# Two up-projections of a scan get buffers of their own; readout weights and gated outputs move to the ring of the scans' loads

## The chip, the core and the metric

The kernel runs on one core of one Trainium2 chip. The metric is device time in microseconds (us) of one execution. Engines: PE is TensorE, DVE VectorE, ACT ScalarE, POOL GpSimd, SP SyncE, which here issues nearly all DMA transfers, in its program's order.

## The reference

Two blocks on 256 tokens of width 2048, in float32, batch 1. The first block is two layers of attention (four kinds of head groups). The second, which the change lies in, is one trunk layer: the latent tokens (x) and 256 context tokens (c) are projected with the same weights, a pair of recurrent branches reads both, their results are merged, and an MLP follows.

```
h  = modulate(rms_norm_2(x, norm1_w), sh1, sc1)
hc = modulate(rms_norm_2(ctx, norm1_w), csh1, csc1)
p, pc = h @ in_w, hc @ in_w[:, :A_COLS + B_COLS]
pa, pb, pg = split_cols(p, [A_COLS, B_COLS, GATE_COLS])
ya = rwkv7_branch(pa, pca, ...)      # 16 heads of 64
yb = gdn_branch(pb, pcb, ...)        # 8 heads of 128, gated delta rule
x = x + g1 * merge_branches(ya, yb, pg, up_a, up_b, out_w)
x = x + g2 * squared_relu_mlp(modulate(rms_norm_2(x, norm2_w), sh2, sc2), mlp_w1, mlp_w2)

def rwkv7_prepare(z, w0, w_up, a0, a_up, k_k, k_a):
    ...
    tw = jnp.tanh(xw)
    for d in range(2):
        w = -jax.nn.softplus(-(w0[d] + tw @ w_up[d])) - 0.5
        a = jax.nn.sigmoid(a0[d] + xa @ a_up[d])
        k_d = k * (1.0 + (a - 1.0) * k_a)
    ...

def merge_branches(ya, yb, pg, up_a, up_b, out_w):
    gate_a, gate_b = jnp.split(jax.nn.sigmoid(pg), 2, axis=-1)
    return (gate_a * (ya @ up_a) + gate_b * (yb @ up_b)) @ out_w
```

Each scan goes over the context first and hands its state to the scan over x; only the scans over x give an output. `w_up` and `a_up` (here `wup` and `aup`) are the two up-projections of the RWKV branch. An RWKV output is normalised per head with `ln_w` and `ln_b` and multiplied by a gate from `g_up`; a gated output is normalised per head and gated.

## The kernel before, in words

All weights of the projections are streamed: `load_w` (L140) loads tiles `wr` of 512 KB into three buffers, ACT splits each into a rounded part `wh` (L230) and DVE the rest `wl` (L231), and PE multiplies them with the activations in three products (L171 to L173, in PSUM tiles `pp`). These matmuls fill PE for nearly the whole time.

The scans run beside the projections. There are twelve, each a Python generator: four RWKV scans on c (`rwkv`, four heads each), two gated ones on c (`gdn`, also four heads each), then four and two on x. `scans` keeps two of them going at a time, in two slots, and takes the next when one ends. The four RWKV scans on x are called x0 to x3 in this document. The projection of the gates and `up_a` (the multiplication of `ya` with its up-projection) come at the end of the stretch in which the scans run, then `merge`, which begins with loading the gated result `ytb` from DRAM (L1711). Each branch's output goes to DRAM: `yad` (L1455) for RWKV, from where `up_a` loads it as `yk` (L1699), `ybd` (L1652) for the gated one.

The order of the instructions on each engine is not written by hand. A scheduler places them by priority (the scans' is raised by 4000 against that of the code beside them) and by its own estimate of times. A tile name with several buffers is a ring: a new tile takes a buffer that is free, and its first write, here the load on SP, waits until the last reader of what lay there is done. SP issues in its program's order, so whatever stands behind such a load waits as well.

The ring "p2" has N2 = 5 buffers of 128x512 float32. An RWKV scan takes from it k2, v2, on x also r2 (in the trace `k`, `v` and `r`), `wup` and `aup`; a gated scan takes two `gvt` and a `gsq`. All loads of `_load` stand on L1405, whatever asked for them. Each (direction, head pair) of an RWKV scan multiplies first with `wup` (L1233), then with `aup` (L1234). L1221 transposes v2; L1273 makes `kr` from k2 and r2, and is their last reader.

The name "lg" has one buffer of 128x1024. The readout of an RWKV scan on x puts its normalisation weights (`ln`) and `gup` there; a gated scan on x gathers its output there as `gosb` (L1610 to L1641), from which L1649 transposes head by head, L1651 multiplies with the gate (`go`), and L1652 stores.

Of the kernel before, what the change touches and what calls it, by code (L numbers as in the profile page):

```python
# [13 lines left out]
AF = mybir.ActivationFunctionType  # L14
# [3 lines left out]
MUL, ADD, SUB = ALU.mult, ALU.add, ALU.subtract  # L18
# [11 lines left out]
N1, N2, NM = 6, 5, 4  # L30
# [20 lines left out]
def bc(ap, n, axis):  # L51

    l = [list(x) for x in ap.ap]
    l.insert(axis, [0, n])
    return bass.AP(tensor=ap.tensor, offset=ap.offset, ap=l)
# [787 lines left out]
class Second:  # L843
# [337 lines left out]
    def rwkv(self, b, src):  # L1181
        e, nc, a = self.e, self.e.nc, self.a
        v, s, g = nc.vector, nc.scalar, nc.gpsimd
        mm, tr = nc.tensor.matmul, nc.tensor.transpose
# [4 lines left out]
        f256 = slice(256 * b, 256 * b + 256)  # L1189
        ld = lambda n, ap: self._load(n, ap, "p2")  # L1190
        k2, v2 = ld("k2", zd[:, 8 + t0:10 + t0, :]), ld("v2", zd[:, 16 + t0:18 + t0, :])
        r2 = ld("r2", zd[:, t0:t0 + 2, :]) if isx else None
        wu = ld("wup", a["wup"][:, :, f256].rearrange("d p c -> p d c"))
        au = ld("aup", a["aup"][:, :, f256].rearrange("d p c -> p d c"))
        cols = lambda n: pv[n][:, t0:t0 + 2]

        hk, ok, hkk = (e.t([128, 2], n, 2) for n in ("hk", "ok", "hkk"))
# [6 lines left out]
        p = e.pt()  # L1204
        for t in range(2):
            sq = e.t([128, T], "sq", N1, tag="p1")
# [11 lines left out]
        p = e.pt()  # L1218
# [9 lines left out]
        for t in range(2):  # L1228
            fs = []
            for d in range(2):  # L1230
                p = e.pt()
# [31 lines left out]
                f = e.t([128, T], "rf", N1, tag="p1")  # L1263
# [6 lines left out]
            if isx:  # L1270
# [3 lines left out]
                f = e.t([128, T], "rf", N1, tag="p1")  # L1274
# [138 lines left out]
    def rwkv_readout(self, b, yT, bo, vn):  # L1413
        e, nc, a = self.e, self.e.nc, self.a
        v, s, g = nc.vector, nc.scalar, nc.gpsimd
        lg = e.t([128, 2, 2, 256], "lg", 1)
        ln, gup = lg[:, 0], lg[:, 1]
        for n in range(2):
            nc.sync.dma_start(ln[:, n], bc(a[("lnw", "lnb")[n]][256 * b:256 * b + 256], 128, 0))
        nc.sync.dma_start(gup, a["gup"][:, :, 256 * b:256 * b + 256])  # L1420
        p = e.pt()
        py = p.rearrange("p (i t r c) -> p i t r c", i=2, t=2, r=2)
        for i in range(2):
            for t in range(2):
                nc.tensor.transpose(py[:, i, t].rearrange("p r c -> p (r c)"), yT[:, t, i, :], e.ident)
        y = e.t([128, 2, 2, 2, 64], "ynat", NN, tag="nat")
        m = e.t([128, 2, 2, 2], "ym", 1)
        v.tensor_reduce(m, py, axis=AX.X, op=ADD)
        f3 = lambda x: x.rearrange("p i t r -> p (i t r)")
        v.tensor_scalar(f3(m), f3(m), 1.0 / 64, None, op0=MUL)  # L1430
        yf = y.rearrange("p i t r c -> p (i t r) c")
        v.tensor_tensor(yf, p.rearrange("p (u c) -> p u c", c=64), bc(f3(m), 64, 2), op=SUB)
        sq = e.t([128, 8, 64], "ysq", NN, tag="nat")
        s.activation(sq, yf, AF.Square)
        ss = e.t([128, 8], "yss", 1)
        v.tensor_reduce(ss, sq, axis=AX.X, op=ADD)
        r = e.t([128, 8], "yrs", 1)
        e.rsqrt(r, ss, [128, 8], "y", 1.0 / 64, 64e-5)
        v.tensor_tensor(yf, yf, bc(r, 64, 2), op=MUL)
        y2 = y.rearrange("p i t r c -> p i (t r c)")  # L1440
        v.tensor_tensor(y2, y2, bc(ln[:, 0], 2, 1), op=MUL)
        v.tensor_tensor(y2, y2, bc(ln[:, 1], 2, 1), op=ADD)
        v.tensor_tensor(sq, vn.rearrange("p i t (r c) -> p (i t r) c", r=2), bc(f3(bo), 64, 2), op=MUL)
        v.tensor_tensor(yf, yf, sq, op=ADD)
        for t in range(2):
            p = e.pt()
            for k in range(2):
                nc.tensor.matmul(p[:, :T], gup[:, k, t * 128:(t + 1) * 128], self.xg[:, k, :], start=k == 0, stop=k == 1)
            for i in range(2):
                nc.tensor.transpose(p[:, T + i * 128:T + (i + 1) * 128], y[:, i, t].rearrange("p r c -> p (r c)"), e.ident)  # L1450
            gt = e.t([128, T], "rgt", N1, tag="p1")
            s.copy(gt, p[:, :T])
            o = e.t([128, T], "ro", N1, tag="p1")
            v.tensor_tensor(o, p[:, T:], gt, op=MUL)
            nc.sync.dma_start(self.ya[:, 2 * b + t, :], o)  # L1455
# [35 lines left out]
    def gdn(self, b, src):  # L1491
# [81 lines left out]
        S = e.t([128, 2, 4, 128], "gst", 2, tag="vs")  # L1573
        if isx:
            nc.sync.dma_start(S, self.gstd[b])
            osb = e.t([128, 2, 4, 128], "gosb", 1, tag="lg")
        cc = lambda h: slice(h * 128, h * 128 + 128)
        p3 = lambda p: p.rearrange("p (h c) -> p h c", h=4)
        for j in range(2):
            blk = (j, 1 - j)  # L1580
            first = not isx and j == 0
            for d in range(2):
                i = blk[d]
                c = slice(i * 128, (i + 1) * 128)
                col = lambda x, h: x[:, i, d * 8 + h0 + h:d * 8 + h0 + h + 1]
                if isx:
                    at = self._load("gatl", self.at[:, d, b * 8 + i * 4:b * 8 + i * 4 + 4, :], "mk")
                if first:
                    rhs = vn[:, i]
                else:  # L1590
                    p = e.pt()
                    for h in range(4):
                        mm(p[:, cc(h)], kq[:, h, 0, c], S[:, d, h, :], start=True, stop=True)
                    rhs = e.t([128, 4, 128], "grhs", 1, tag="ysb")
                    for h in range(4):
                        v.scalar_tensor_tensor(rhs[:, h], p[:, cc(h)], col(negeg, h), vn[:, i, h], op0=MUL, op1=ADD)
                p = e.pt()
                for h in range(4):
                    mm(p[:, cc(h)], nt[:, d, i * 4 + h, :], rhs[:, h], start=True, stop=True)
                y = e.t([128, 4, 128], "gyy", NM, tag="mk")  # L1600
                v.tensor_tensor(y, p3(p), bc(m[:, i, d], 128, 2), op=MUL)
                if isx:
                    pa, pb = e.pt(), e.pt()
                    for h in range(4):
                        mm(pa[:, cc(h)], kq[:, h, 1, c], S[:, d, h, :], start=True, stop=True)
                        mm(pb[:, cc(h)], at[:, h], y[:, h], start=True, stop=True)
                    o = osb[:, i]
                    t1 = o if j == 0 else e.t([128, 4, 128], "gt1", NN, tag="nat")
                    for h in range(4):
                        s.activation(t1[:, h], pa[:, cc(h)], AF.Copy, scale=col(eg, h))  # L1610
                    if j:
                        v.tensor_tensor(o, o, t1, op=ADD)
                    v.tensor_tensor(o, o, p3(pb), op=ADD)
                if not (isx and j):
                    y2 = e.t([128, 4, 128], "gy2", NN, tag="nat")
                    v.tensor_tensor(y2, y, bc(ee[:, i, d * 8 + h0:d * 8 + h0 + 4], 128, 2), op=MUL)
                    p = e.pt()
                    for h in range(4):
                        mm(p[:, cc(h)], kn[:, i, h], y2[:, h], start=True, stop=True)
                    if first:  # L1620
                        s.copy(S[:, d], p3(p))
                    else:
                        for h in range(4):
                            v.scalar_tensor_tensor(S[:, d, h], S[:, d, h], col(gend, h), p[:, cc(h)], op0=MUL, op1=ADD)
                yield
# [3 lines left out]

        qn = e.t([128, 2, 4], "gqn", 1, tag="ym")  # L1630
        v.tensor_scalar(f2(qn), f2(rn[:, 1]), 128 ** -0.5, None, op0=MUL)
        of = osb.rearrange("p i h c -> p (i h) c")
        v.tensor_tensor(of, of, bc(f2(qn), 128, 2), op=MUL)
        os_ = e.t([128, 8], "gos", 1, tag="yss")
        for i in range(2):
            sq = e.t([128, 4, 128], "gsq2", NN, tag="nat")
            s.activation(sq, osb[:, i], AF.Square)
            v.tensor_reduce(os_[:, i * 4:i * 4 + 4], sq, axis=AX.X, op=ADD)
        r = e.t([128, 8], "gor", 1, tag="yrs")
        e.rsqrt(r, os_, [128, 8], "go", 1.0 / 128, EPS)  # L1640
        v.tensor_tensor(of, of, bc(r, 128, 2), op=MUL)  # L1641
        gw = e.t([128, 1], "ggw", 1)
        v.tensor_scalar(gw, self.pv["gnw"], 0.5, None, op0=MUL)
        for h in range(4):
            gt = e.t([128, T], "ggt", N1, tag="p1")
            nc.sync.dma_start(gt, self.gz[:, h0 + h, :])
            p = e.pt()
            for i in range(2):
                tr(p[:, i * 128:(i + 1) * 128], osb[:, i, h], e.ident)  # L1649
            o = e.t([128, T], "go", N1, tag="p1")  # L1650
            v.scalar_tensor_tensor(o, p[:, :T], gw, gt, op0=MUL, op1=MUL)  # L1651
            nc.sync.dma_start(self.yb[:, h0 + h, :], o)  # L1652
# [285 lines left out]
```

## Time and profile before

| | |
|---|---|
| median of 3 runs | 3415.12 us (3408.39 to 3417.45) |
| the profiled execution | 3419.12 us, its span 3417.4 us |
| PE busy | 3287.1 us (96%) |
| DVE busy | 2360.5 us (69%) |
| ACT busy | 1591.9 us (47%) |
| granted PE clock, mean | 0.975 of 2.4 GHz |
| the chain that ended last | PE 83%, DMA 9%, DVE 5% |

The time of the profiled execution is its span and 1.7 us around it. Busy shares are sums over the span; the chain is followed back from the last instruction, at each step to what released it. The rows on which the prediction rests stand below.

### The profile page before, as it was taken

Reading aid. Unit: us, or ns where it says so; the run is one execution under the profiler, and the core shown is the slowest. Engines: PE = TensorE matmul, PEld = TensorE weight load, DVE = VectorE, ACT = ScalarE, POOL = GpSimd, SP = SyncE. Lnnn points to the kernel's source line nnn. Section 1 sums busy time; section 2 is a strip of 40 time slices with the busy share of each in tenths; the row PEclk is TensorE's granted clock in tenths of the full one; section 3 lists DMA queues with packets and bytes.
Section 4 is the critical chain, followed back from the end, with each engine's and each line's share of the span. In section 5 each row is a group of like instructions: output and inputs, shape, how many; then the busy total and the mean of one; then the engine's idle time right before and its main releaser. Section 6 shows DMA issues by size and latency. Waiting matters only on the chain.

```text
span 3417.4 us, 76977 instructions
## 1 busy us (share of the span) xinstructions
PE 3287.1 (96%) x30462; PEld 3015.2 (88%) x30462; DVE 2360.5 (69%) x5128; ACT 1591.9 (47%) x3191; POOL 352.9 (10%) x635
## 2 busy tenths in 40 slices
PE   8999999999999999999989989999989999999998
PEld 6878889878789898989988889999888989899987
DVE  7757766567577697978887677577767555556655
ACT  4444455443444564635444244245345545445553
POOL 1101000001011030201111103002020000001000
PEclk9999999999999998989999998999999999999999
DMA  7676776876765562535444244255555785555554
GB/s 251 219 257 236 258 233 209 270 263 202 258 206 170 188 191 86 161 100 166 146 151 151 77 146 143 79 174 173 158 189 196 246 272 188 188 188 183 184 189 154
DMA packets 224822, 640.73 MB, mean 187 GB/s; under 512 B 24330, under 2 KB 79948, under 8 KB 224332
## 3 DMA queue, kind: packets, MB, share of 16 engines
q1 hardware_dynamic: 224460, 635.81, 56.9%
q8 instruction: 239, 3.92, 0.5%
q14 instruction: 123, 1.01, 0.1%
HBM read 607.78 MB, written 27.93 MB: 186 GB/s over the span
## 4 chain that ended last, share of the span: by engine, by line
PE 83%; DMA 9%; DVE 5%; issue 1%; ACT 1%; POOL 0%; SPq 0%; DVEq 0%; ACTq 0%
PE pp L173 16%; PE pp L171 16%; PE pp L172 16%; PE pp L166 7%; DMA mw<-in_mod_w 4%; PE pp L167 4%; PE mps L891 3%; PE pp L204 2%; PE pp L203 2%; PE pp L205 2%; DVE wl L231 2%; DMA wup<-in_wup 1%; PE sm L1291 1%; PE sm L1321 1%; PE sm L1333 1%
## 5 line engine op out<-in xcount | busy, mean ns | idle before, releaser
L231 DVE TENSOR_TENSOR wl<-wr,wh 128x512 fp32r<-128x512 f32 x1752 | 1220.8, 703 | 690.3 <-ACT wh L230 664.1
L230 ACT CAST wh<-wr 128x512 fp32r<-128x512 f32 x1752 | 1075.5, 619 | 1300.3 <-PE pp L172 831.9
L171 PE MATMUL pp<-act,wh 128*128 128x256 f32 x3920 | 1133.2, 290 | 19.3 <-ACT wh L230 10.3
L173 PE MATMUL pp<-act,wl 128*128 128x256 f32 x3920 | 1130.1, 289 | 2.4 <-DVE wl L231 2.4
L172 PE MATMUL pp<-act,wh 128*128 128x256 f32 x3920 | 1129.1, 288 | 0.0
L171 PEld LDWEIGHTS pp<-act,wh 128*128 128x128 f32 x3920 | 759.8, 194 | 44.5 <-ACT wh L230 16.0
L173 PEld LDWEIGHTS pp<-act,wl 128*128 128x128 f32 x3920 | 759.1, 194 | 21.5 <-issue 9.7
L172 PEld LDWEIGHTS pp<-act,wh 128*128 128x128 f32 x3920 | 760.4, 194 | 12.6 <-issue 8.5
L173 PE MATMUL pp<-mhi,wl 128*128 128x258 f32 x1024 | 291.5, 285 | 0.0
L171 PE MATMUL pp<-mhi,wh 128*128 128x258 f32 x1024 | 290.4, 284 | 0.0
L172 PE MATMUL pp<-mlo,wh 128*128 128x258 f32 x1024 | 288.5, 282 | 0.0
L166 PE MATMUL pp<-act,wh 128*128 128x512 f32 x752 | 266.0, 396 | 0.0
L167 PE MATMUL pp<-act,wl 128*128 128x256 f32 x768 | 212.4, 280 | 0.8 <-DVE wl L231 0.8
L171 PEld LDWEIGHTS pp<-mhi,wh 128*128 128x128 f32 x1024 | 194.6, 190 | 4.5 <-ACT wh L230 3.7
L173 PEld LDWEIGHTS pp<-mhi,wl 128*128 128x128 f32 x1024 | 193.2, 189 | 4.1 <-issue 4.1
L172 PEld LDWEIGHTS pp<-mlo,wh 128*128 128x128 f32 x1024 | 194.5, 190 | 0.5 <-issue 0.4
L166 PEld LDWEIGHTS pp<-act,wh 128*128 128x128 f32 x752 | 141.2, 188 | 31.6
L166 PE MATMUL pp<-u,wh 128*128 128x512 f32 x480 | 168.2, 392 | 0.0
L167 PEld LDWEIGHTS pp<-act,wl 128*128 128x128 f32 x768 | 144.7, 188 | 4.6 <-DVE wl L231 1.7
L891 PE MATMUL mps<-mw,scw 128*32 128x256 f32 x1536 | 121.7, 390 | 17.9 <-DMA mw<-in_mod_w 17.6
L167 PE MATMUL pp<-u,wl 128*128 128x256 f32 x512 | 138.0, 280 | 0.0
L166 PEld LDWEIGHTS pp<-u,wh 128*128 128x128 f32 x480 | 90.1, 188 | 20.2
(529 smaller groups left out, 4631.4 us busy)
## 6 DMA issues: line engine op xcount, KB each, us to landing
wr<-in_in_w SPq DMA_DIRECT2D x252, 512.0 KB, 4.1
wr<-in_w SPq DMA_DIRECT2D x240, 512.0 KB, 4.6
mw<-in_mod_w SPq DMA_DIRECT2D x192, 512.0 KB, 6.0
wr<-in_w1m SPq DMA_DIRECT2D x128, 512.0 KB, 4.0
wr<-in_w2m SPq DMA_DIRECT2D x128, 512.0 KB, 3.5
wr<-in_wo SPq DMA_DIRECT2D x64, 512.0 KB, 4.5
wr<-in_out_w SPq DMA_DIRECT2D x32, 512.0 KB, 3.2
wr<-in_up_a SPq DMA_DIRECT2D x16, 512.0 KB, 3.2
```

Source lines behind the costliest of these rows:

```text
L166: mm(o, hi, h[2][:, k, :], start=k == 0, stop=False)
L167: mm(o[:, :T], lo, h[0][:, k, :], start=False, stop=False)
L171: mm(o, hi, h[0][:, k, :], start=k == 0, stop=False)
L172: mm(o, hi, h[1][:, k, :], start=False, stop=False)
L173: mm(o, lo, h[0][:, k, :], start=False, stop=k == nk - 1)
L203: mm(p[b], x, hi, start=k == 0, stop=False)
L204: mm(p[b], x, wlo, start=False, stop=False)
L205: mm(p[b], xl, hi, start=False, stop=k == nk - 1)
L230: self.nc.scalar.copy(hi, sl)
L231: self.nc.vector.tensor_tensor(lo, sl, hi, op=SUB)
L891: nc.tensor.matmul(ps[32 * j:32 * j + 32], self.scw[:, k, :], w[:, j * 256:(j + 1) * 256], start=k == 0, stop=k == NK - 1, tile_position=( ...
L1291: mm(p4(p)[:, d, t, :], bT[rows[r], t, d, ch[i]], ar[rows[r], t, d, 0, ch[i]], start=True, stop=True)
```

## The change

`wup` and `aup` leave the ring "p2": each gets a name of its own with one buffer. The shared tile "lg" goes. `ln` and `gup` become two tiles of the ring "p2", and `gosb` two tiles of 128x512 of that ring, one for each half of the tokens. The two multiplies over all of `gosb` (before L1633 and L1641) become two each, on half the size. N2 stays 5.

```diff
--- before.py
+++ after.py
@@ -1190,8 +1190,8 @@
         ld = lambda n, ap: self._load(n, ap, "p2")
         k2, v2 = ld("k2", zd[:, 8 + t0:10 + t0, :]), ld("v2", zd[:, 16 + t0:18 + t0, :])
         r2 = ld("r2", zd[:, t0:t0 + 2, :]) if isx else None
-        wu = ld("wup", a["wup"][:, :, f256].rearrange("d p c -> p d c"))
-        au = ld("aup", a["aup"][:, :, f256].rearrange("d p c -> p d c"))
+        wu = self._load("wup", a["wup"][:, :, f256].rearrange("d p c -> p d c"))
+        au = self._load("aup", a["aup"][:, :, f256].rearrange("d p c -> p d c"))
         cols = lambda n: pv[n][:, t0:t0 + 2]
 
         hk, ok, hkk = (e.t([128, 2], n, 2) for n in ("hk", "ok", "hkk"))
@@ -1413,8 +1413,7 @@
     def rwkv_readout(self, b, yT, bo, vn):
         e, nc, a = self.e, self.e.nc, self.a
         v, s, g = nc.vector, nc.scalar, nc.gpsimd
-        lg = e.t([128, 2, 2, 256], "lg", 1)
-        ln, gup = lg[:, 0], lg[:, 1]
+        ln, gup = (e.t([128, 2, 256], n, N2, tag="p2") for n in ("ln", "gup"))
         for n in range(2):
             nc.sync.dma_start(ln[:, n], bc(a[("lnw", "lnb")[n]][256 * b:256 * b + 256], 128, 0))
         nc.sync.dma_start(gup, a["gup"][:, :, 256 * b:256 * b + 256])
@@ -1573,7 +1572,7 @@
         S = e.t([128, 2, 4, 128], "gst", 2, tag="vs")
         if isx:
             nc.sync.dma_start(S, self.gstd[b])
-            osb = e.t([128, 2, 4, 128], "gosb", 1, tag="lg")
+            osb = [e.t([128, 4, 128], f"gosb{i}", N2, tag="p2") for i in range(2)]
         cc = lambda h: slice(h * 128, h * 128 + 128)
         p3 = lambda p: p.rearrange("p (h c) -> p h c", h=4)
         for j in range(2):
@@ -1604,7 +1603,7 @@
                     for h in range(4):
                         mm(pa[:, cc(h)], kq[:, h, 1, c], S[:, d, h, :], start=True, stop=True)
                         mm(pb[:, cc(h)], at[:, h], y[:, h], start=True, stop=True)
-                    o = osb[:, i]
+                    o = osb[i]
                     t1 = o if j == 0 else e.t([128, 4, 128], "gt1", NN, tag="nat")
                     for h in range(4):
                         s.activation(t1[:, h], pa[:, cc(h)], AF.Copy, scale=col(eg, h))
@@ -1629,16 +1628,17 @@
 
         qn = e.t([128, 2, 4], "gqn", 1, tag="ym")
         v.tensor_scalar(f2(qn), f2(rn[:, 1]), 128 ** -0.5, None, op0=MUL)
-        of = osb.rearrange("p i h c -> p (i h) c")
-        v.tensor_tensor(of, of, bc(f2(qn), 128, 2), op=MUL)
+        for i in range(2):
+            v.tensor_tensor(osb[i], osb[i], bc(qn[:, i], 128, 2), op=MUL)
         os_ = e.t([128, 8], "gos", 1, tag="yss")
         for i in range(2):
             sq = e.t([128, 4, 128], "gsq2", NN, tag="nat")
-            s.activation(sq, osb[:, i], AF.Square)
+            s.activation(sq, osb[i], AF.Square)
             v.tensor_reduce(os_[:, i * 4:i * 4 + 4], sq, axis=AX.X, op=ADD)
         r = e.t([128, 8], "gor", 1, tag="yrs")
         e.rsqrt(r, os_, [128, 8], "go", 1.0 / 128, EPS)
-        v.tensor_tensor(of, of, bc(r, 128, 2), op=MUL)
+        for i in range(2):
+            v.tensor_tensor(osb[i], osb[i], bc(r[:, i * 4:i * 4 + 4], 128, 2), op=MUL)
         gw = e.t([128, 1], "ggw", 1)
         v.tensor_scalar(gw, self.pv["gnw"], 0.5, None, op0=MUL)
         for h in range(4):
@@ -1646,7 +1646,7 @@
             nc.sync.dma_start(gt, self.gz[:, h0 + h, :])
             p = e.pt()
             for i in range(2):
-                tr(p[:, i * 128:(i + 1) * 128], osb[:, i, h], e.ident)
+                tr(p[:, i * 128:(i + 1) * 128], osb[i][:, h], e.ident)
             o = e.t([128, T], "go", N1, tag="p1")
             v.scalar_tensor_tensor(o, p[:, :T], gw, gt, op0=MUL, op1=MUL)
             nc.sync.dma_start(self.yb[:, h0 + h, :], o)
```

The change moves instructions on every engine in the stretch of the scans, since the scheduler decides anew. Three places:

SP's queue around the load of x1's up-projections, from the program of before. `zx` are columns of the projection on their way to the scans, `gstd` is a state that a gated context scan stores, k_28806 is the k2 of x2; what a row waits for stands in brackets, by engine or DMA queue.

```order
L987 DMA zx<-zsh 128x256 [waits DMAHW7_49,DVE_49]
L140 DMA wr<-in_in_w 128x1024 [waits DMAHW4_49,DMAHW0_49,DVE_49]
L1627 DMA gstd_13484<-gst 128x1024 [waits DMAHW1_49,DVE_49]
L1405 DMA wup<-in_wup 97x2x256 [waits DMAHW2_49,DVE_49]
L1405 DMA aup<-in_aup 128x2x256
L1405 DMA k_28806<-zx 128x512 [waits PE_49]
L140 DMA wr<-in_in_w 128x1024 [waits DMAHW5_49,DVE_49]
```

The same place after the change; r_27370 is x1's own r2.

```order
L1405 DMA r_27370<-zx 128x512 [waits DMAHW7_49,DMAHW4_49,PE_49]
L140 DMA wr<-in_in_w 128x1024 [waits DMAHW3_49,DVE_49]
L140 DMA wr<-in_in_w 128x1024 [waits DMAHW5_49,DVE_49]
L140 DMA wr<-in_in_w 128x1024 [waits DMAHW0_49,DVE_49]
L987 DMA zx<-zsh 128x256 [waits DVE_49]
L140 DMA wr<-in_in_w 128x1024 [waits DMAHW6_49,DMAHW2_49,DVE_49]
L140 DMA wr<-in_in_w 128x1024 [waits DMAHW3_49,DVE_49]
L1405 DMA wup<-in_wup 97x2x256 [waits PE_49]
L1405 DMA aup<-in_aup 128x2x256 [waits DMAHW1_49,PE_49]
```

Before, `wup` waits for an instruction of DVE (L1273 of x0); now it waits for one of PE, the last L1233 of x0. From that one to x1's first L1233 PE has 197 matmuls in the old order and 217 in the new. For x3 the release was PE's L1221 of x3 itself, 36 matmuls ahead of the first L1233, and is now x2's last L1233, 325 ahead.

PE's queue at the end of up_a and the begin of the merge, before the change. `act` is `ya` and `yb` the gated result, both split into parts; `pp` are the projections.

```order
L171 MATMUL pp<-act_32233,wh 128x256
L172 MATMUL pp<-act_32233,wh 128x256
L173 MATMUL pp<-act_32233,wl 128x256
L1649 MATMUL sm<-ident,gosb 128x128 x8
L171 MATMUL pp<-yb_32876,wh 128x256 x3
L172 MATMUL pp<-yb_32876,wh 128x256
```

The last transposes of the second gated scan after the change:

```order
L171 MATMUL pp<-act_32243,wh 128x256
L1649 MATMUL sm<-ident,gosb_32010 128x128
L1649 MATMUL sm<-ident,gosb_32011 128x128
L172 MATMUL pp<-act_32243,wh 128x256
L173 MATMUL pp<-act_32243,wl 128x256
L171 MATMUL pp<-act_32236,wh 128x256
```

Before, the merge's first matmul on `yb` stands right behind the last transpose; now 122 matmuls of up_a stand between the two.

SP's queue where up_a's input is loaded, before the change; `ua` takes the gates from DRAM:

```order
L1032 DMA gated<-zsh 128x256
L1699 DMA yk<-yad 128x256 x2
L1687 DMA ua_32241<-gated 128x256
L1699 DMA yk<-yad 128x256 x2
L1405 DMA gatl<-atd 128x512
L1699 DMA yk<-yad 128x256 x4
```

And after it:

```order
L1646 DMA ggt<-gzd 128x256
L1652 DMA ybd<-go 128x256
L1687 DMA ua_32250<-gated 128x256
...
L1646 DMA ggt<-gzd 128x256
L1652 DMA ybd<-go 128x256
L1687 DMA ua_32251<-gated 128x256
L1699 DMA yk<-yad 128x256
L1646 DMA ggt<-gzd 128x256
L1699 DMA yk<-yad 128x256 x2
L1652 DMA ybd<-go 128x256
```

The loads of `yk` now stand among the gate loads (`ggt`) and stores (`ybd`) of the first gated scan on x, which before stood behind them.

## Rows read from the trace of the kernel before

**Rows 1.** The page: the span, and each engine's busy time and share.
```profile
span 3417.4 us, 76977 instructions
PE 3287.1 (96%) x30462; PEld 3015.2 (88%) x30462; DVE 2360.5 (69%) x5128; ACT 1591.9 (47%) x3191; POOL 352.9 (10%) x635
```

**Rows 2.** PE's waits, 1100 to 2520 us: us in total, times, longest.
```profile
PE sm L1233 <- DMA wup<-in_wup: 25.4, 4, 9.4
PE pp L171 <- DMA ytb<-ybd: 13.3, 1, 13.3
PE pp L171 <- ACT wh L230: 6.5, 2, 3.9
...
PE pp L171 <- ACT act L305: 4.4, 1, 4.4
...
PE pp L171 <- DVE ua L1688: 1.8, 1, 1.8
```

**Rows 3.** Busy time, clock and DMA share by stretch of the span.
```profile
core 0: us, PE busy (x) PEld busy (x) DVE busy (x) ACT busy (x) POOL busy (x), PEclk, DMA share, GB/s
1713.20:1738.90 25.70, 25.70 (x217) 25.48 (x215) 24.70 (x76) 14.71 (x31) 3.98 (x5) 1.00 0.50 164
...
1748.40:1758.50 10.10, 10.10 (x40) 8.99 (x40) 5.12 (x17) 1.08 (x4) 0.00 (x0) 0.50 0.13 50
1758.50:1768.60 10.10, 10.10 (x87) 9.90 (x87) 9.21 (x28) 6.84 (x17) 0.00 (x0) 1.00 0.27 82
...
1988.20:2030.90 42.70, 42.68 (x350) 42.21 (x348) 37.02 (x98) 25.23 (x54) 0.00 (x0) 1.00 0.61 189
...
2039.90:2058.90 19.00, 19.00 (x77) 17.02 (x78) 9.60 (x30) 4.05 (x10) 0.00 (x0) 0.50 0.10 35
...
2510.60:2516.30 5.70, 5.67 (x26) 5.67 (x27) 4.01 (x11) 2.23 (x7) 0.00 (x0) 0.50 0.09 32
```

**Rows 4.** Timeline of SP's queue in x1 and x3: start us, us, issue.
```profile
1736.06 0.25 SPq L1405 DMA_DIRECT2D wup<-in_wup  x1
1736.36 5.80 SPq L1405 DMA_DIRECT2D aup<-in_aup  x1
...
2027.30 0.28 SPq L1405 DMA_DIRECT2D wup<-in_wup  x1
```

**Rows 5.** Timeline of DVE, just before that load in x1.
```profile
1735.56 0.47 DVE L1273 SCALAR_TENSOR_TENSOR kr<-k,pv,r 128x256 f32<-128x256 f32 x1
```

**Rows 6.** Timeline of PE around L1233; idle time before and its releaser in brackets.
```profile
1162.28 1.22 PE L1233 MATMUL sm<-twec,wup 97*128 97x256 f32 x2 [5.88 <-DMA wup<-in_wup]
...
1712.55 0.59 PE L1233 MATMUL sm<-twex,wup 97*128 97x256 f32 x2
...
1748.37 2.05 PE L1233 MATMUL sm<-twex,wup 97*128 97x256 f32 x4 [9.42 <-DMA wup<-in_wup]
...
2025.85 0.63 PE L1221 MATMUL sm<-ident,v 128*128 128x128 f32 x4
...
2039.86 1.62 PE L1233 MATMUL sm<-twex,wup 97*128 97x256 f32 x3 [8.98 <-DMA wup<-in_wup]
```

**Rows 7.** The tile `aup`: its issues on SP, ns shortest/median/longest.
```profile
L1405 SPq DMA_DIRECT2D aup<-in_aup x8: 385/5186/6548, 1149.2 to 2033.4; - x8
```

**Rows 8.** Timeline of PE where the merge begins.
```profile
2496.51 0.83 PE L1649 MATMUL sm<-ident,gosb 128*128 128x128 f32 x4 [1.27 <-DVE go L1651]
2510.63 1.01 PE L171 MATMUL pp<-yb,wh 128*128 128x256 f32 x3 [13.29 <-DMA ytb<-ybd]
```

**Rows 9.** The tile `gosb`: durations in ns, shortest/median/longest.
```profile
L1613 DVE TENSOR_TENSOR gosb<-gosb,sm x8: 666/688/689, 2392.9 to 2481.6; 128x512 f32<-128x512 f32 x8
...
L1633 DVE TENSOR_TENSOR gosb<-gosb,gqn x2: 1219/1222/1226, 2419.9 to 2482.8; 128x1024 f32<-128x1024 f32 x2
L1641 DVE TENSOR_TENSOR gosb<-gosb,gor x2: 1225/1226/1226, 2433.5 to 2493.3; 128x1024 f32<-128x1024 f32 x2
```

## The prediction

> **What bounds the kernel now.** I read the page first. TensorE (PE) is busy for 3287.1 of 3417.4 us [rows 1], so all its idle time together is 130 us, and a change that leaves its matmuls alone can only win part of that, and what the low clock after an idle spell costs. Then I asked for PE's waits in the stretch of the scans alone, 1100 to 2520 us [rows 2]. The reader is to see which tiles this change can touch: 25.4 us in four waits for `wup`, 13.3 us in one wait for `ytb`, the load of the gated rule's result at the start of the merge, and, in a row of PE's timeline, 1.27 us for `go`, the step before its store [rows 8]. That is 40.0 us. Third, one row for each stretch of the clock [rows 3]. After each long wait the granted clock is 0.50, which is 1.2 of 2.4 GHz: PE issues 40 matmuls in the 10.10 us behind the second wait and 87 in the next 10.10 us, at 1.00. So a wait costs itself and about half of the slow stretch behind it.
>
> **Why `wup` comes late.** Call the latent scans x0 to x3. In x1 the issue of `wup` stands at 1736.06 us [rows 4], right after `kr` (L1273) of x0, at 1735.56 us [rows 5]. `kr` is the last reader of k2 and r2, and `wup` needs a buffer of the ring "p2" that one of these holds. PE comes to x1's first L1233 and sits 9.42 us, until 1748.37 us [rows 6]; from issue to use that is 12.31 us. x0's own last use of its `wup` was over at 1712.55 + 0.59 = 1713.14 us [rows 6]: the weights wait not for their own predecessor but for the ring. In x3 the same: `wup` issued at 2027.30 us [rows 4] behind the transposes of v2 (L1221, from 2025.85 us), wait 8.98 us, use at 2039.86 us, 12.56 us after the issue [rows 6]. The first context scan waits 5.88 us, with no scan ahead of it [rows 6]; the four sum to 25.4, so the fourth wait is 25.4 - 9.42 - 8.98 - 5.88 = 1.1 us, in x0.
>
> **The change part by part.** *Up-projections with a buffer each.* Now `wup` waits only for the last L1233 of the scan before. For x1 the new order puts 217 matmuls between that and the first use; the old order had 197 there, and they took 25.70 us at full clock, from 1713.20 to 1738.90 us [rows 3] (217 records, since a scan's own matmuls leave two each). The load needs 12.31 us, so it is covered with some 13 us to spare. For x3 the new order has 325 matmuls between, the old one 341, which took 42.70 us [rows 3]: about 40 us against 12.56. x0's load moves ahead by more than that: it now waits only for the last context scan's L1233. The first context scan keeps its 5.88 us: its issue stands at the same place. So the terms are:
> x1: 9.42 + half of 10.10 = 14.5 us. x3: 8.98 + half of 19.00 = 18.5 us. x0: 1.1 us.
> From below, each is zero if something else of the scan comes as late; I take the whole, since nothing else of the scan was late: in x3 the transposes of v2 had run 14 us before the wait ended [rows 6].
>
> A rule speaks against this part. The Trainium skill ("Trainium Kernel Development and Optimization", Best Practices) says to double-buffer so that loads overlap compute, and these tags get one buffer. The row agrees only in part: one buffer forbids a load during the scan that uses it, but between the last use and the next first use lie 25.70 us [rows 3]. By the rule the two waits would stay, and the time would be that of rival 2; by the row they go.
>
> *What else is on SP's queue.* The instruction behind `wup` takes long to issue, `aup` a median of 5.2 us (5186 ns) [rows 7], and the weight loads `wr` stand behind it. Twice before PE waited for the split of such a weight, 6.5 us in two, longest 3.9 [rows 2]. The new order has the pair at the same number of places, eight, so I count neither gain nor loss; the bounds are -6.5 and +6.5.
>
> *Readout weights in the ring.* `ln` and `gup` take buffers of "p2", so the next k2, v2 and r2 may wait for a readout. I followed the new order for every load of the scans, counting PE's matmuls between what releases the load and the first instruction that needs it. Before, the shortest two of the scans on x are `wup` of x1 and x3 (53 and 36 matmuls). In the new order the shortest of the ring's loads on x are `gup` of the last readout (162) and r2 of x3 (165); by the 25.70 us for 197, that is 21 us against the 12.56 that the slowest load took. Under 60 stand only two `gatl`, the gated rule's own loads, at the very end (57 and 56); they speak for rival 1. I cost this part at nothing; without that cover each such load would cost what x1's cost, 14.5 us.
>
> *The gated rule's outputs as two ring tiles.* `gosb` shared one buffer with the readouts' weights, so the second gated scan on x could not write its output before the first had transposed its own. In the new order it does, and its last transpose (L1649) stands 122 matmuls ahead of the merge's first, instead of right ahead of it. Before, the last L1649 started at 2496.51 us, with a wait of 1.27 us, and the merge's first L171 at 2510.63 us after 13.29 us of waiting [rows 8]. 122 of up_a's matmuls at 0.12 us each (217 records in 25.70 us) are 14.6 us: just the 14.1 us between those two rows. So the wait goes, with nothing to spare; then 5.70 us at 0.50 [rows 3] go as well.
> Tail: 13.29 + 1.27 + half of 5.70 = 17.4 us.
>
> *What this pulls in.* The up_a matmuls that covered the second gated scan before now stand behind it. Where the gates' projection ends and up_a begins, 36 matmuls of the scans stand alone, and the loads of `yk`, which up_a needs, stand on SP behind four stores of the first scan's output. Before, the same hand-over cost 4.4 us (`act` L305) and 1.8 us (`ua` L1688) [rows 2]. The bounds are 0 and the 13.29 us of the wait it replaces; the nearest row is the 4.4, since it is the same wait for the same `yk`. I take 4 us more than before.
>
> *Split multiplies.* A 128x1024 multiply is 1222 or 1226 ns, a 128x512 one 688 [rows 9]: two for one cost 0.15 us more, four times, 0.6 us, on DVE, which idles 31%. Half of it may lie on the last scan's path: 0.3 us.
>
> **Sum.** 14.5 + 18.5 + 1.1 + 17.4 = 51.5, less 4 and 0.3 is 47 us. The profiled execution took 3419.12 us, which gives 3372; the median of the runs is 3415.12, 4 us less, which gives 3368. I forecast 3370.
>
> **The rivals.**
> 1. *The tail gives its part back.* The wait at the merge is replaced by one at up_a's start: the last gated scan without cover, `yk` behind the stores, the clock at 0.50. For it: 14.6 against 14.1 us leaves no slack, and what is pulled ahead of up_a loses its cover. Against it: before, the scans ran beside the gates' projection at 1.00. Gain 14.5 + 18.5 + 1.1 - 4 = 30: 3387 us.
> 2. *The `wup` waits stay or move*, to the weight behind `aup`, or since one buffer is too few. For it: the 5.2 us of issue, and the 3.9 us wait. Against it: 25.70 us of cover. Only the tail gains, 17.4 - 4.3 = 13: 3404 us.
> 3. *Slower: the ring runs dry.* Five buffers now hold a scan's loads, two tiles for each readout and four for the gated rule's outputs. If k2, v2 or r2 come as late as `wup` did, each costs 9 us and 5 to 9.5 us of slow clock, some 16.5. An SP queue that waits for a ring buffer also holds the `wr` loads behind it. For it: before, the queue did wait so, for `kr`. Against it: the counts above. It decides from three such loads (3 x 16.5 = 49.5, all of the gain); with four of them 51.5 - 66 - 4 = -18.5: 3436 us. The Trainium skill ("DMA: Bandwidth & Descriptors", Anatomy of one DMA) says that a transfer's semaphore wait happens on the issuing sequencer, before dispatch. By that rule a ring wait stops every load behind it; the 12.31 us between a `kr` and its use are that, so the trace agrees.
> 4. *Nothing much:* waits move and the sum is within 10 us.
>
> **How the numbers follow.** My forecast has 0.55 (its own range 3354 to 3382), rival 1 0.18, rival 2 0.13, rival 3 0.06, rival 4 0.08. The median is the forecast's. Runs of before spread from 3408.39 to 3417.45, so 0.3%, 10 us, is about what can be told from no change. Rival 2 lies near that bound, 13 us with a few us of doubt: I put 0.11 of it on faster and 0.02 on same. Faster: 0.55 + 0.18 + 0.11 = 0.84; same 0.10; slower 0.06. The range runs from 3354, where the hand-over is free and a weight wait goes too (3368 - 4 - 6.5, and a few for what I left out), to 3402, which takes in rival 1 and part of rival 2; outside lie rivals 3 and 4, half of 2, and little below.
>
> **What would show it.** Right: `wup` gone from PE's waits but for the 5.9 us in the first context scan; clock at 1.00 behind x1's and x3's first L1233; PE going from up_a to the merge without a `ytb` wait over 2 us. Wrong: a new wait for v2, k2 or r2, `wh` L230 waits of more than 6.5 us, or more than 10 us before the first `act` of up_a. The forecast fails most easily at the tail, where 14.6 us must cover 14.1.

## The result and the profile after

The changed kernel takes 3365.86 us (median of 4 runs, 3362.18 to 3373.88), against 3413.75 us before (median of 4: the three runs of the table above and one more): a ratio of 0.9856, with a 95% interval from 0.9832 to 0.9881. The two profiled executions are 3419.12 and 3366.81 us, 52.3 us apart.

The page of the changed kernel, span and busy time, which answers to [rows 1]:

```profile
span 3365.1 us, 76958 instructions
PE 3266.7 (97%) x30462; PEld 2997.4 (89%) x30462; DVE 2358.3 (70%) x5132; ACT 1588.5 (47%) x3191; POOL 347.6 (10%) x635
```

PE has the same 30462 records and is busy 20.5 us less: the same matmuls, more of them at the full clock (the mean granted clock rose from 0.975 to 0.985). Its idle time fell from 130.3 to 98.4 us, 31.9 us. The two together are the 52.3 us.

PE's waits of the changed kernel from 1100 to 2480 us, in the columns of [rows 2]:

```profile
PE pp L171 <- ACT wh L230: 13.5, 4, 5.9
PE sm L1233 <- DMA wup<-in_wup: 5.8, 1, 5.8
...
PE pp L171 <- ACT act L305: 1.7, 1, 1.7
```

Only the first context scan still waits for `wup`. No wait for `ytb` is left. But the waits for a weight's split (`wh`, L230) have doubled, from 6.5 us in two to 13.5 in four; 10.7 of these lie in the stretch of the context scans, 2.6 before.

Where along the run the time went is read from stretches between the same instructions in both kernels: the first L1233 of the first context scan, the first L1233 of x0, the last L1233 of x3, the merge's first L171 on `yb`. Of before (columns as [rows 3]):

```profile
1162.28:1688.25 525.97, 506.11 (x6593) 481.96 (x6594) 442.54 (x1177) 271.71 (x584) 89.68 (x209) 0.95 0.46 144
1688.25:2082.60 394.35, 370.24 (x3753) 349.49 (x3754) 295.05 (x759) 173.59 (x373) 55.39 (x113) 0.94 0.43 135
2082.60:2510.60 428.00, 403.99 (x4949) 382.64 (x4947) 292.72 (x699) 168.78 (x371) 52.69 (x131) 0.96 0.47 147
```

and of the changed kernel:

```profile
1158.49:1694.10 535.61, 508.60 (x6624) 483.94 (x6625) 443.44 (x1177) 272.28 (x586) 87.75 (x208) 0.95 0.46 144
1694.10:2051.60 357.50, 351.22 (x3696) 332.31 (x3695) 291.33 (x752) 168.88 (x366) 48.16 (x102) 0.99 0.45 143
2051.60:2460.00 408.40, 400.99 (x4976) 381.29 (x4974) 290.50 (x701) 167.20 (x372) 57.09 (x142) 0.99 0.49 152
```

The context scans lost 9.6 us. From x0 to x3 36.9 us were won, and the clock went from 0.94 to 0.99. From x3 to the merge it was 19.6 us. The counts show that matmuls also changed place: 57 records fewer in the middle stretch, 31 and 27 more beside it, at 0.12 us each some 7, 4 and 3 us. Before the first of these instructions lie 3.8 us: PE stood idle 17.9 us ahead of its products with `mw`, weights that the change does not touch, and 14.1 us in the changed kernel (13.9 to 19.3 us over all the profiled executions). Behind the last lie 1.7 us.

Two rows of the changed kernel's PE timeline show the merge, as [rows 8] did before:

```profile
2444.45 0.41 PE L1649 MATMUL sm<-ident,gosb 128*128 128x128 f32 x2
...
2460.01 0.39 PE L171 MATMUL pp<-yb,wh 128*128 128x256 f32 x1 [0.51 <-ACT yb L305]
```

15.6 us lie between the last two transposes and the merge, filled with up_a's matmuls; the wait is 0.51 us in place of 13.29.

What the context scans lost is seen at x0's pair of loads, which now follows the last context scan's use at once. SP's queue of the changed kernel:

```profile
1397.66 0.25 SPq L1405 DMA_DIRECT2D wup<-in_wup  x1
1398.09 5.25 SPq L1405 DMA_DIRECT2D aup<-in_aup  x1
1403.39 0.63 SPq L1013 DMA_DIRECT2D gcd<-zsh  x1
1404.12 1.37 SPq L140 DMA_DIRECT2D wr<-in_in_w  x3
```

and PE's timeline just behind it:

```profile
1412.11 0.58 PE L171 MATMUL pp<-act,wh 128*128 128x256 f32 x1 [5.91 <-ACT wh L230]
```

The issue behind `wup` holds SP for 5.25 us, three weight tiles are issued late, and PE waits 5.91 us for the first. Where the load of `wup` is made quick and stands at the same place, that wait is gone (below, "The slow load itself").

The clock behind the first L1233 of x1 and of x3 in the changed kernel, over as many us as the slow stretches of [rows 3] had:

```profile
1747.38:1757.48 10.10, 10.10 (x77) 9.24 (x76) 8.61 (x31) 5.96 (x16) 0.00 (x0) 1.00 0.75 240
2019.56:2038.56 19.00, 19.00 (x151) 18.14 (x150) 17.55 (x57) 10.30 (x25) 0.00 (x0) 1.00 0.49 163
```

### The profile page after: what moved, and what is told of

It is laid out like the page before. It is cut to its first block, busy times and chain, and to the rows that moved or that the text cites. A ratio compares the mean times of both kernels' runs of the same rounds, so it can differ in the third digit from the quotient of the medians.

```text
span 3365.1 us, 76958 instructions
## 1 busy us (share of the span) xinstructions
PE 3266.7 (97%) x30462; PEld 2997.4 (89%) x30462; DVE 2358.3 (70%) x5132; ACT 1588.5 (47%) x3191; POOL 347.6 (10%) x635
## 4 chain that ended last, share of the span: by engine, by line
PE 85%; DMA 7%; DVE 5%; issue 1%; ACT 1%; POOL 0%; SPq 0%; DVEq 0%; ACTq 0%
PE pp L171 17%; PE pp L173 17%; PE pp L172 17%; PE pp L166 8%; PE pp L167 4%; DMA mw<-in_mod_w 3%; PE mps L891 3%; PE pp L204 2%; PE pp L203 2%; PE pp L205 2%; DVE wl L231 1%; PE sm L1291 1%; PE sm L1342 1%; PE sm L1321 1%; PE sm L1333 1%
## 5 line engine op out<-in xcount | busy, mean ns | idle before, releaser
L230 ACT CAST wh<-wr 128x512 fp32r<-128x512 f32 x1752 | 1074.5, 619 | 1293.3 <-PE pp L172 818.7
L171 PE MATMUL pp<-act,wh 128*128 128x256 f32 x3920 | 1133.1, 290 | 23.7 <-ACT wh L230 18.0
L171 PEld LDWEIGHTS pp<-act,wh 128*128 128x128 f32 x3920 | 758.6, 194 | 50.1 <-ACT wh L230 24.1
L171 PE MATMUL pp<-mhi,wh 128*128 128x258 f32 x1024 | 290.7, 284 | 0.0
L171 PEld LDWEIGHTS pp<-mhi,wh 128*128 128x128 f32 x1024 | 194.8, 190 | 4.5 <-ACT wh L230 3.7
L891 PE MATMUL mps<-mw,scw 128*32 128x256 f32 x1536 | 122.0, 391 | 14.1 <-DMA mw<-in_mod_w 13.9
```

What stands on the lines that cost most here:

```text
L171: mm(o, hi, h[0][:, k, :], start=k == 0, stop=False)
L230: self.nc.scalar.copy(hi, sl)
L891: nc.tensor.matmul(ps[32 * j:32 * j + 32], self.scw[:, k, :], w[:, j * 256:(j + 1) * 256], start=k == 0, stop=k == NK - 1, tile_position=( ...
```

## The experiments

Each is compared with the kernel before, run beside it on the same chip (its medians there: 3414.88 us for the first two and for those on the slow load and on `aup` ahead of `wup`, 3418.70 for the cut in 89 and 8 and for the ring half with the cut, 3416.52 for the rest). Two questions: is the gain two gains, the `wup` waits and the tail, as predicted? And why does a load of 194 KB take 12 us?

**One half alone: the ring.** The change with the two loads put back into the ring:

```diff
-        wu = self._load("wup", a["wup"][:, :, f256].rearrange("d p c -> p d c"))
-        au = self._load("aup", a["aup"][:, :, f256].rearrange("d p c -> p d c"))
+        wu = ld("wup", a["wup"][:, :, f256].rearrange("d p c -> p d c"))
+        au = ld("aup", a["aup"][:, :, f256].rearrange("d p c -> p d c"))
```

> Readout weights and gated outputs in the ring as in the change, but wup and aup stay in the ring too. Theory of the prediction (two separate gains): the wup waits of x1 and x3 stay, the wait for ytb at the merge goes for its own reason, the two tiles of gosb; about 13 us below the kernel before, 3400 us. Rival (one gain: the tail was late only because the scans were late through wup): the order here has the last transposes 15 rows ahead of the merge and not 122, so the wait for ytb stays over 8 us and the time is within 6 us of the kernel before, 3408 to 3420.

3399.33 us, ratio 0.9945 (0.9925 to 0.9965). By the median the prediction's theory had the number, but the profile, of an execution of 3413.33 us, has the rival's rows. PE's waits:

```profile
PE sm L1233 <- DMA wup<-in_wup: 24.4, 4, 9.4
PE pp L171 <- DMA ytb<-ybd: 11.2, 1, 11.2
```

With `gosb` in two tiles the wait for `ytb` is still 11.2 us; 14 matmuls lie between the last transposes and the merge:

```profile
2491.83 0.38 PE L1649 MATMUL sm<-ident,gosb 128*128 128x128 f32 x2
2505.11 1.01 PE L171 MATMUL pp<-yb,wh 128*128 128x256 f32 x3 [11.23 <-DMA ytb<-ybd]
```

Why the other three executions (3391 to 3400 us) were quicker than this one can't be read from it; that stays open.

**The other half, without a buffer of its own.** The kernel before with one number changed:

```diff
-N1, N2, NM = 6, 5, 4
+N1, N2, NM = 6, 6, 4
```

> The kernel before with one number changed, six buffers in the ring for five: wup and aup stay in it, lg stays shared. Theory of the prediction: the wup waits of x1 and x3 go, the wait for ytb stays at 13 us, 33 us below before, 3380 us. Rival (one gain): with the scans no longer late both go although gosb is one shared tile, 45 to 50 us below before, 3364 to 3369. A third, that wup needs a buffer of its own: nothing changes, 3413.

3365.44 us, ratio 0.9859 (0.9839 to 0.9878): the whole gain of the change. `gosb` is one shared tile as before, and no wait for `ytb` is among PE's waits; for `wup` there is

```profile
PE sm L1233 <- DMA wup<-in_wup: 7.1, 2, 5.8
```

At the merge 122 matmuls lie between the last transpose and the first product, as in the changed kernel:

```profile
2451.09 0.41 PE L1649 MATMUL sm<-ident,gosb 128*128 128x128 f32 x2
...
2466.23 0.39 PE L171 MATMUL pp<-yb,wh 128*128 128x256 f32 x1
```

So the tail's wait goes with the ring's relief, not with the tiles of `gosb`.

**The own buffers, lg as before.** The first two lines of the change alone; the ring has four buffers so that all fits.

```diff
-N1, N2, NM = 6, 5, 4
+N1, N2, NM = 6, 4, 4
...
-        wu = ld("wup", a["wup"][:, :, f256].rearrange("d p c -> p d c"))
-        au = ld("aup", a["aup"][:, :, f256].rearrange("d p c -> p d c"))
+        wu = self._load("wup", a["wup"][:, :, f256].rearrange("d p c -> p d c"))
+        au = self._load("aup", a["aup"][:, :, f256].rearrange("d p c -> p d c"))
```

> The kernel before with buffers of their own for wup and aup, lg shared as before, and a ring of four (five do not fit beside lg). Prediction's theory (the tail needs the two tiles of gosb): 30 to 33 us below before, a wait for ytb of about 13 us. Rival (one gain, the tail follows the scans): 45 to 50 us below, no ytb wait over 2 us. With four buffers r2 of x1 and x3 is released 68 and 26 matmuls ahead of its use: a wait there of a few us would show the ring running dry.

3376.04 us, ratio 0.9877 (0.9846 to 0.9909), which alone lies between the two. The profile decides, of an execution of 3366.69 us, the quickest of the four: there is no wait for `ytb` here either, 121 matmuls lie ahead of the merge, and the 68 and 26 matmuls for r2 cost nothing that shows among PE's waits. In it the ring did not run dry at four.

**The slow load itself.** The changed kernel with `wup`'s load in two pieces; the order of the rest is the same.

```diff
-        wu = self._load("wup", a["wup"][:, :, f256].rearrange("d p c -> p d c"))
+        wsrc = a["wup"][:, :, f256].rearrange("d p c -> p d c")
+        wu = e.t([97, 2, 256], "wup", 1)
+        nc.sync.dma_start(wu[:96], wsrc[:96])
+        nc.sync.dma_start(wu[96:97], wsrc[96:97])
```

> The changed kernel with the load of wup cut in two, 96 partitions and the 97th; the order of all else is the same. Theory: it is wup's 97 partitions that make the next issue on SP take 5 us and the load land after 12: the issue behind falls under 1 us, the landing under 6, the four waits for wh L230 (13.5 us) fall to under 4 and the first wup wait of 5.8 us under 2, with the clock behind them: 15 to 20 us below the changed kernel, 3346 to 3351. Rival: SP's issue is slow because of the queue's length at that moment, whatever the shape: the issue behind stays near 5 us and the time within 5 us of the changed kernel.

3331.97 us, ratio 0.9756 (0.9738 to 0.9773), by the ratios 34 us below the changed kernel, and the fastest here: twice what was expected. In the profile 6 us of it lie at the first pair, 17 in the context scans and 9 between x0 and x3. SP's queue at the first pair, in the changed kernel and with the cut:

```profile
1145.12 0.29 SPq L1405 DMA_DIRECT2D wup<-in_wup  x1
1145.45 6.56 SPq L1405 DMA_DIRECT2D aup<-in_aup  x1
...
1143.33 0.42 SPq L1195 DMA_DIRECT2D wup<-in_wup  x1
1143.80 0.73 SPq L1196 DMA_DIRECT2D wup<-in_wup  x1
1144.57 0.40 SPq L1408 DMA_DIRECT2D aup<-in_aup  x1
```

`aup` issues in 0.40 us in place of 6.56; no wait for `wup` and none over 1 us for `wh` is left. What the long load did is best seen in the DMA's rate in 40 slices around the first pair. The changed kernel, 1145 to 1158.5 us:

```profile
GB/s 255 291 291 279 279 303 285 413 310 127 67 36 24 24 24 24 24 21 24 24 24 24 55 152 273 343 352 349 273 252 200 279 237 267 249 285 246 279 328 416
```

and with the cut, 1143 to 1150.7 us:

```profile
GB/s 213 128 340 213 340 362 255 340 341 224 298 287 181 256 351 372 362 240 208 271 383 362 357 271 229 303 410 356 298 372 335 372 415 383 383 362 436 309 388 362
```

For some 3.5 us the whole core moves 24 GB/s: SP is held by the issue of `aup` from 1145.45 to 1152.01 us, so nothing new is issued, what was in flight has landed, and `wup` alone is left. At 24 GB/s its 194 KB would take 8.3 us (an estimate from these two numbers). The share of the 16 DMA engines that is busy (the column before the rate) is 0.07 in that stretch, where one engine of 16 would make 0.06; with the cut it is 0.99:

```profile
1149.00:1152.00 3.00, 3.00 (x28) 3.00 (x27) 3.00 (x4) 1.68 (x4) 2.33 (x3) 1.00 0.07 24
...
1143.30:1150.70 7.40, 7.40 (x66) 7.40 (x65) 7.14 (x19) 3.74 (x9) 6.23 (x9) 1.00 0.99 322
```

The Trainium skill ("DMA: Bandwidth & Descriptors", Why a DMA increments its semaphore by 16 and not by 1) states that a transfer is spread over the largest number of engines, up to 16, that divides the size of the slowest dimension (of more than one element) of both its source and its destination. By that rule, as an estimate, 97 partitions go to one engine, 96 to all. The share of 0.07 and the effect of the cut agree with that.

**Is it the partitions, or two transfers for one?** As above, in 89 and 8:

```diff
-        nc.sync.dma_start(wu[:96], wsrc[:96])
-        nc.sync.dma_start(wu[96:97], wsrc[96:97])
+        nc.sync.dma_start(wu[:89], wsrc[:89])
+        nc.sync.dma_start(wu[89:97], wsrc[89:97])
```

> The changed kernel with wup cut in two as in the third experiment, but in 89 and 8 partitions; the order is the same. If it is the number of partitions that makes the load slow, 89 being a prime as 97 is, the issue behind stays at 4 to 6 us, the first wup wait at 5 us or more and the time within 8 us of the changed kernel, 3358 to 3374. If two transfers for one were what helped, it is with the cut at 96, 3327 to 3337.

3359.67 us, ratio 0.9831 (0.9801 to 0.9860). The long issue is back, now on the second piece:

```profile
1145.38 0.29 SPq L1195 DMA_DIRECT2D wup<-in_wup  x1
1145.70 6.29 SPq L1196 DMA_DIRECT2D wup<-in_wup  x1
```

The first wait for `wup` is back too, 5.7 us. It is the number of partitions, and not that there are two transfers. Which numbers beside 97 and 89 are slow, no run here tells.

**`aup` ahead of `wup`.** The two lines exchanged.

> The changed kernel with aup issued ahead of wup. If wup is the cause of the long issue behind it, aup issues in under 1 us and the long issue of 5 us falls on the instruction behind wup, a weight or a column; time within 5 us of the changed kernel. If aup itself is slow to issue, wup behind it stays short and nothing else becomes long.

3368.52 us, ratio 0.9860 (0.9843 to 0.9877). The scheduler put `wup` first again in seven of eight places, so this tells little. In the one where `aup` led, the long issue fell on the instruction behind `wup`:

```profile
1138.90 0.43 SPq L1405 DMA_DIRECT2D aup<-in_aup  x1
1139.37 0.33 SPq L1405 DMA_DIRECT2D wup<-in_wup  x1
1139.74 7.28 SPq L1405 DMA_DIRECT2D k<-zc  x1
```

The kernel before has such a place too. At x3 a weight stands right behind `wup`; it takes 5.65 us, and `aup` behind it 0.39:

```profile
2027.30 0.28 SPq L1405 DMA_DIRECT2D wup<-in_wup  x1
2027.67 5.65 SPq L140 DMA_DIRECT2D wr<-in_in_w  x1
2033.42 0.39 SPq L1405 DMA_DIRECT2D aup<-in_aup  x1
```

So whatever stands behind `wup` is held, and not `aup` for itself. Nor is it a wait that the program asks for: x1's `aup` before, of 5.80 us [rows 4], has none in brackets in the first order shown under "The change".

**The cut without the change.** The kernel before, `wup` still in the ring of five:

```diff
-        wu = ld("wup", a["wup"][:, :, f256].rearrange("d p c -> p d c"))
+        wsrc = a["wup"][:, :, f256].rearrange("d p c -> p d c")
+        wu = e.t([97, 2, 256], "wup", N2, tag="p2")
+        nc.sync.dma_start(wu[:96], wsrc[:96])
+        nc.sync.dma_start(wu[96:97], wsrc[96:97])
```

> The kernel before with only the load of wup cut in 96 partitions and the 97th; its order is that of before, the ring has five buffers and lg stays shared. If the slow load is the root and the ring only made it show, the waits of x1 and x3 shrink from 9 us each to under 3, the first from 5.9 to under 1, the wh L230 waits to under 2; the wait for ytb at the merge stays at 13 us, since its order is that of before: 40 to 45 us below before, 3370 to 3375. Rival (the ring is the root): the waits of x1 and x3 stay over 6 us; 10 to 20 us below before.

3363.21 us, ratio 0.9842 (0.9818 to 0.9866): as much as the change, with the order of before, and some 10 us more than was expected. `wup` waits for the ring as it did, but costs 1.0 us in all. The tail, whose order is that of before, is unchanged:

```profile
2440.63 0.98 PE L1652 MATMUL sm<-ident,gosb 128*128 128x128 f32 x4 [1.27 <-DVE go L1654]
2454.90 1.01 PE L171 MATMUL pp<-yb,wh 128*128 128x256 f32 x3 [13.29 <-DMA xold<-x1d]
```

The row names the load of `xold`, another input of the merge, which landed last. It is the wait of before all the same: the first cast of `ytb` (L305), which this product reads, starts at 2454.4 us, just ahead of it.

**The ring half and the cut.** The first experiment with the same cut.

> The first experiment (readout weights and gated outputs in the ring, wup and aup too) with the load of wup cut at 96. With quick loads the change's second half alone: if the two tiles of gosb free the tail, the ytb wait falls under 3 us and the time is 12 us or more below the kernel before with the cut, 3351 or less. If the tail follows the order of the scans, the last transposes here stand 15 rows ahead of the merge, the wait stays at 9 to 13 us, and the time is within 6 us of 3363.

3359.07 us, ratio 0.9829 (0.9804 to 0.9855), within the 6 us of the rival's 3363, and the wait at the merge is still there: 12.71 us in PE's timeline, behind the last transposes that stand 15 rows ahead:

```profile
2451.07 1.01 PE L171 MATMUL pp<-yb,wh 128*128 128x256 f32 x3 [12.71 <-DMA xold<-x1d]
```

**A ring of six and the cut.**

> The ring of six of the second experiment and the cut load of wup together. If the change's own buffers are worth nothing beyond one more place in the ring, this is within 5 us of the changed kernel with the cut, 3327 to 3337; if the own buffers count once the load is quick, it is 10 us or more above.

3340.81 us, ratio 0.9776 (0.9745 to 0.9807), beside 0.9756 (0.9738 to 0.9773) for own buffers with the cut. It lies between the two forecasts, and the intervals overlap; the two can't be told apart.

**Two buffers for `wup`** in the changed kernel, one for `aup`.

> The changed kernel with two buffers for wup, one for aup. By the rule to double-buffer the load of x1 and x3 needs the second buffer, and this is faster by the waits that are left; by the rows one buffer left 25 us of cover, no wup wait but the first is left, and the time is within 5 us of the changed kernel, 3361 to 3371.

3378.51 us, ratio 0.9883 (0.9858 to 0.9909): above the 3361 to 3371 expected, and no gain. In its order the second context scan's `wup` is issued right behind the first pair, and the long issue falls on SP twice in a row there, 6.70 and 8.99 us:

```profile
1150.12 6.70 SPq L1406 DMA_DIRECT2D aup<-in_aup  x1
...
1158.23 0.41 SPq L1194 DMA_DIRECT2D wup<-in_wup  x1
1158.69 8.99 SPq L1406 DMA_DIRECT2D k<-zc  x1
```

The stretch of the context scans takes 545.2 us, 9.5 more than in the changed kernel. The rule to double-buffer, weighed in the prediction, does not pay here: one buffer already left the load its 25 us, and the only `wup` wait left is the first, 5.6 us.

## Why the prediction was right, and where its steps were not

*The time.* 3370 forecast, 3365.86 measured; 47 us of gain forecast, 47.9 by the medians. The range and the sign held.

*x0 to x3: right.* 34.1 us forecast for the three waits with their clock (14.5 + 18.5 + 1.1). From x0 to x3 36.9 us were won, of which some 7 are matmuls that moved to other stretches: 30. Idle time there fell from 24.1 to 6.3 us and busy time by 19.0. The half of each slow stretch was a fair price: the clock rose as forecast, to 1.00 behind x1's and x3's first L1233.

*The tail: near in size, wrong in cause.* The prediction put 17.4 us down to "the gated rule's outputs as two ring tiles". The runs don't bear that out: with the two tiles and `wup` in the ring the wait is 11.2 us, or 12.71 with quick loads; with one shared tile and a ring of six, or own buffers and a ring of four, it is gone. What decides is where the order puts the second gated scan's last transposes against up_a: 121 or 122 matmuls ahead of the merge with each way of relieving the ring, 0 to 15 without. That is shown, also by the kernel before with the quick load: its scans are no longer late, its order is the old one, and the wait is 13.29 us as before. Why the scheduler places the scans so much earlier once the ring is relieved is only argued: its own estimate holds the waits for the ring too.

*The hand-over: wrong.* 4 us more than before were taken; the wait for `act` at up_a's start is 1.7 us where it was 4.4, and with the 3.2 us that PE waits just ahead of it in a gated scan (`gyy`) it is 4.9 us where `act` and `ua` were 6.2. The tail with it won 19.6 us, 23 with the matmuls that moved in, where 13.1 were forecast.

*"The pair at the same number of places, so neither gain nor loss": wrong.* This is where the forecast was short of a loss. The places are eight, but x0's pair moved to right behind the last context scan's, into a stretch where weights have little lead. The `wh` waits rose by 7.0 us, just outside the bound of 6.5, and the context stretch lost 9.6 us, 6 after the matmuls that moved. Rival 2's mechanism was there, beside the gain and not in its place. The prediction's own sign of being wrong, `wh` waits of more than 6.5 us, came with it. The loss here (6), what x0 to x3 fell short of (4) and the surplus at the tail (10) cancel, so that the sum came out better than its steps; that part is luck.

*The ring running dry:* did not happen, at five buffers or at four. The 12.31 us that rival 3 gives for a wait for the ring are something else: they run from the issue of x1's `wup` to its use, when that wait was over. What does show the rule named there is x2's `wup` before, for which SP stood 3.4 us until a `kr` was done, with everything behind it in its queue (SP's waits, 1100 to 2520 us):

```profile
SPq L1405 <- DVE kr L1273: 3.4, 1, 3.4
```

*What lay underneath:* the prediction took the 12 us of the load as given. Cutting it gives 53 us without the change and 83 us with it. Stretches of the profiled executions, in us:

| | before | the change | the cut alone | both |
|---|---|---|---|---|
| first load of `wup`, issue to use | 13.4 | 13.4 | 7.4 | 7.4 |
| context scans | 526.0 | 535.6 | 511.8 | 518.5 |
| x0 to x3 | 394.4 | 357.5 | 359.1 | 348.6 |
| x3 to the merge | 428.0 | 408.4 | 427.4 | 409.0 |

The cut alone wins the waits from x0 to x3 and leaves the tail; what the change adds to it in these stretches is chiefly the tail, 18.4 us, for of the 10.5 us between x0 and x3 some 7 are again matmuls that moved.

## What to carry to other kernels

When a load is waited for, ask first why it takes so long, and only then why it is issued late: here a load of 97 partitions in place of 96 and 1 cost as much as the ring. The issue *behind* a bad transfer is the one that looks slow, and everything else on that queue waits for it. Before two gains are added, run each half alone: here relieving the ring carried both waits. What the two tiles of `gosb` and the readout weights are worth by themselves stays open: 15 us in the first experiment, from executions that left no profile, and 4 us beside the quick load, which is within the noise.

## What the runs showed of the hardware

A load of 97 partitions was used 12.3 to 13.4 us after its issue, and the next issue on its queue, when it followed at once, took 4 to 7 us (9 where two such loads stood close), with the whole core's DMA at 24 GB/s for some 3.5 us of it; behind the same bytes as 96 and 1 it took 0.4 us. In 89 and 8 the second piece takes 3.6 to 6.3 us to issue. With the ring of six a weight issued 1.98 us behind `wup` took 2.98 us, and one issued 6.50 us behind it 0.33: the queue was held for about 5 us from the issue of `wup`, whatever stood next.
